# Weight-stationary fp32r pairs: the low weights' 256 columns first, and the low weights moved by 16 bytes

## The chip, the core and the metric

The kernel runs on one core of a Trainium2 chip. The metric is the device time of one execution in microseconds, as the median of several executions. TensorE is called PE here, VectorE DVE, ScalarE ACT, GpSimd POOL and the engine that issues most transfers SP. A line number such as L154 is a line of the kernel before.

## The reference

Two layers of a causal decoder over 256 positions of width 2048 (fp32): each is a sandwich-normed token mixer and a gated MLP of width 5632 with a causal depthwise convolution of width 3 on the gate.

```python
h = _rmsnorm(x, nrm[0]);  proj = h @ w_in_a[layer]       # layer 0: q, k, v, memory q
...                                                      # dilated attention, 12 heads; memory attention
x = x + _rmsnorm(heads @ w_o, norms[1])
u = _rmsnorm(x, norms[2]) @ w_up;  gate, val = jnp.split(u, 2, axis=-1)
acc = b_conv + ...                                       # 3 taps of the gate
x = x + _rmsnorm((jax.nn.silu(acc) * val) @ w_down, norms[3])
kv = _rmsnorm(x, g_kv) @ w_kv                            # shared by layer 1
q, qm = jnp.split(_rmsnorm(x, nrm[0]) @ w_in_b[lb], [SB_W], axis=-1)
...                                                      # stick-breaking attention, 12 heads; memory attention; same MLP
```

Nearly all of the work is in products of 256 rows with large weight matrices, each of which is read once.

## The kernel before

Each fp32 operand is split into a high and a low part in the type fp32r (hi is the rounded value, made by a cast on ACT at L669; lo the rest, made by a subtraction on DVE at L670). A product is hi·hi + hi·lo + lo·hi. There are two ways to compute it.

*Activations stationary* (`mm3`, L137): three matmuls of 512 moving columns; the weights move.

*Weights stationary* (`ws_mm`, L154): a feature tile of 128 outputs takes 16 k tiles of 128 rows. For each k tile the high weights `whi` are loaded into PE and multiplied with 512 moving columns, the high and the low activations beside each other (H below), and the low weights `wlo` with 256 columns, the high activations alone (L below). Both write one PSUM bank of 512 columns: H the whole of it, L the first 256. `ws_sum` then adds the two halves of the bank: a COPY on ACT (L165) and an addition on DVE (L166).

A feature tile arrives as one transfer (`raw`, 1 MB) and is split in two halves of 8 k tiles, each with a `whi` and a `wlo` of its own out of rings of four. Where a weight tile stands in memory is set by `halves`: tiles of 1088 elements (4352 bytes, a multiple of 256) of which 1024 are used from an offset on. `APART` sets these offsets for the weight-stationary tiles: 16 elements for whi and 4 for wlo, that is 64 and 16 bytes modulo 256. The other users of `halves`, `mem_kv` among them, use offset 0. The moving activations (`hset`) start at a multiple of 1024 bytes for every k tile.

In `ws_mm` H goes first and L second, apart from the last k tile of a bank and, in `ws_beside`, k tile 7 as well (`turn`), where L goes first. So in those places two L and then two H stand beside each other, or H ends the run.

Weight-stationary tiles are used in three places:

- `ws_pair` and `ws_tile`: 60 tiles one after another, the projections of queries and keys, the memory keys of layer 1, and the MLP groups that are done plainly.
- `ws_beside`: 96 tiles as a generator that `wide` steps through. `wide` computes a group of 512 gate and 512 value columns from sums of blocks (seven products instead of eight), eight units long, twelve such loops in all. Everything in it is recorded in program order (`pin`). In one unit PE runs: the first half of the tile (16 matmuls), products 1, 2 and 3 (nine matmuls at L137), the second half of the tile (16), products 7, 5, 6 and 4 (twelve). After a tile's second half come its `ws_sum` and then the two splits of the next tile, in this order on ACT and on DVE.
- `mem_kv`: the memory keys of layer 0, four banks at once, 64 k tiles with both weights at offset 0.

PE has one queue of instructions, in this order, and each matmul has a weight load of its own ahead of it (PEld in the profile). A matmul whose operand or bank isn't ready holds everything behind it.

Of the kernel before, what the change touches and what calls it, by code (L numbers as in the profile page):

```python
# [11 lines left out]
F32R = mybir.dt.float32r  # L12
# [5 lines left out]
P = 128  # L18
D = 2048
S = 256  # L20
# [4 lines left out]
KT = D // P  # L25
# [11 lines left out]
WIDE = (1, 3, 5, 7, 9)  # L37


APART = (16, 4)  # L40


QK_ORDER = []
# [5 lines left out]
class Body:  # L49
# [10 lines left out]
        return self.psp.tile([P, 512], F32, name="ps_" + tag, tag=tag, bufs=4)  # L60

    def small(self, n, dtype=F32):
        return self.sb.tile([P, n], dtype, name="small", tag="small", bufs=11)

    def sc(self, shape):
        return self.sb.tile(shape, F32, name="sc", tag="sc", bufs=4)
# [36 lines left out]
    def halves(self, at=(0, 0)):  # L103

        both = []
        for name, o in zip(("whi", "wlo"), at):
            both.append(self.sb.tile([P, 1088], F32R, name=name, tag=name, bufs=4)[:, o:o + 1024])
        return both

    def piece(self, src, cuts=1, store=None, between=None, at=(0, 0)):  # L110
# [31 lines left out]
    def ws_tile(self, out, src, h):  # L142
# [3 lines left out]
        self.step()  # L146
        for half, (whi, wlo) in enumerate(self.piece(src, at=APART)):
            for k in range(8):
                self.ws_mm(b, whi, wlo, k, h, half * 8 + k)
        self.ws_sum(out, b)  # L150

    def ws_mm(self, b, whi, wlo, k, h, kt, turn=None):

        mm = lambda *o, **kw: self.pin(self.nc.tensor.matmul(*o, **kw))  # L154
        ks = slice(k * P, (k + 1) * P)
        both, one = h[2][:, kt, :, :].rearrange("p a t -> p (a t)"), h[0][:, kt, :]
        last = kt == KT - 1 or kt == turn
        if not last:
            mm(b, whi[:, ks], both, start=kt == 0, stop=False)
        mm(b[:, 0:S], wlo[:, ks], one, start=False, stop=False)  # L160
        if last:
            mm(b, whi[:, ks], both, start=False, stop=kt == KT - 1)

    def ws_sum(self, out, b):
        self.pin(self.nc.scalar.copy(out, b[:, S:]))  # L165
        self.pin(self.nc.vector.tensor_add(out, b[:, 0:S], out))  # L166

    def ws_beside(self, out, src, h, done=None):


        raw = self.sb.tile([P, 2048], F32, name="raw", tag="raw", bufs=3)
        self.pin(self.nc.sync.dma_start(raw, src))
        parts = []
        for i in range(2):
            parts.append(self.halves(APART))
            self.split(*parts[i], raw[:, i * 1024:(i + 1) * 1024])
            yield
        b = self.bank("s")
        for half, (whi, wlo) in enumerate(parts):
            for k in range(8):  # L180
                self.ws_mm(b, whi, wlo, k, h, half * 8 + k, 7)
            yield
        self.ws_sum(out, b)
        if done:
            done()
# [474 lines left out]
    def rest_of(self, make):  # L660

        halves, rest = [], {}
        for u in range(0, 6, 2):
            rest[u] = lambda u=u: halves.append(make(5 + u // 2))
            rest[u + 1] = lambda: halves.pop()()
        return rest
# [732 lines left out]
```

## Time and profile before

| | |
|---|---|
| median of three executions | 2162.28 us (2161.65 to 2162.35) |
| profiled execution | 2161.4 us |
| span in it, first to last instruction | 2159.6 us |
| granted clock of PE, mean | 0.999 |
| busy: PE, PEld, DVE, ACT, POOL | 99%, 84%, 80%, 62%, 8% |
| moved by DMA | 538.83 MB, mean 250 GB/s |

The rows of the profile have a line, an engine, an operation, what is written and what is read, the shape, the number of instructions, their busy time and mean duration, and the idle time of the engine just before them with what ended it. In the timeline a row has its start and its duration, both in us from the span's start. Matmul records overlap: a matmul's recorded duration is longer than its distance to the next one's start, and a matmul that waits for its weights is recorded as running, so that idle time of PE doesn't always show as such.

### The profile page before, as it was taken

The numbers are of one execution on the slowest core, as the hardware profiler recorded it, in microseconds if no ns is written. First come the engines' busy times: TensorE is split into PE (matmuls) and PEld (weight loads), VectorE is DVE, ScalarE is ACT, GpSimd is POOL, SyncE is SP. The second block draws the span as 40 slices with busy tenths as digits, with TensorE's granted clock in tenths as the row PEclk, the third lists the DMA queues.
The fourth block names the chain that finished last, engine by engine and source line by source line (L and its number), as shares of the span: only waits on it lengthen the run. The fifth ranks groups of instructions, "written<-read, shape, count | busy, mean of one in ns | idle before, by whom it ended". The sixth has DMA issues, their size and how long they took to land.

```text
span 2159.6 us, 29240 instructions
## 1 busy us (share of the span) xinstructions
PE 2146.0 (99%) x10926; PEld 1823.1 (84%) x10926; DVE 1732.9 (80%) x2350; ACT 1328.2 (62%) x1896; POOL 175.4 (8%) x201
## 2 busy tenths in 40 slices
PE   9999999999999999999999999999999999999998
PEld 8888888888888888888888888878888888888887
DVE  7798867997887868788888978579978878687886
ACT  6666756666665666666675655456666656666563
POOL 0000001010101011010111000010101010110110
PEclk9999999999999999999999999999999999999999
DMA  9886557796979889797788744577969798897974
GB/s 371 252 262 247 174 187 259 223 284 220 299 234 283 266 236 303 225 290 257 264 268 260 256 165 177 192 234 229 275 233 288 235 283 269 236 303 222 290 247 184
DMA packets 111775, 538.83 MB, mean 250 GB/s; under 512 B 11280, under 2 KB 11664, under 8 KB 73488
## 3 DMA queue, kind: packets, MB, share of 16 engines
q1 hardware_dynamic: 75744, 445.66, 57.4%
q0 software_dynamic: 35744, 91.24, 20.9%
q8 instruction: 86, 1.41, 0.2%
q14 instruction: 57, 0.47, 0.1%
q10 hardware_dynamic: 144, 0.06, 0.0%
HBM read 510.17 MB, written 26.74 MB: 249 GB/s over the span
## 4 chain that ended last, share of the span: by engine, by line
PE 97%; DVE 1%; issue 1%; ACT 0%; DMA 0%; POOL 0%; POOLq 0%; DVEq 0%; SPq 0%; ACTq 0%
PE ps_g L137 40%; PE ps_s L154 25%; PE ps_g L154 15%; PE ps_s L137 12%; PE ps_s L961 1%; PE ps_s L287 1%; PE ps_s L363 0%; PE ps_s L390 0%; DMA sh<-in_uw_dram 0%; DVE wlo L670 0%; PE ps_s L1082 0%; PE ps_s L495 0%; PE ps_s L477 0%; PE ps_s L535 0%; PE ps_s L434 0%
## 5 line engine op out<-in xcount | busy, mean ns | idle before, releaser
L670 DVE TENSOR_TENSOR wlo<-raw,whi 128x1024 fp32r<-128x1024 f32 (+1 forms) x758 | 855.2, 1151 | 245.7 <-ACT whi L669 232.4
L669 ACT CAST whi<-raw 128x1024 fp32r<-128x1024 f32 (+1 forms) x758 | 742.8, 995 | 386.9 <-PE ps_g L137 145.8
L154 PE MATMUL ps_s<-h,whi 128*128 128x512 f32 x1600 | 573.3, 393 | 0.0
L137 PE MATMUL ps_g<-whi,sh 128*128 128x512 f32 x1488 | 462.0, 392 | 0.5 <-ACT sc L779 0.5
L154 PE MATMUL ps_s<-h,wlo 128*128 128x256 f32 x1600 | 416.2, 280 | 0.1
L154 PEld LDWEIGHTS ps_s<-h,whi 128*128 128x128 f32 x1600 | 300.3, 188 | 54.2
L154 PE MATMUL ps_g<-h,whi 128*128 128x512 f32 x960 | 338.0, 396 | 0.8 <-DVE h L277 0.8
L137 PEld LDWEIGHTS ps_g<-whi,sh 128*128 128x128 f32 x1488 | 277.4, 188 | 57.6 <-ACT sc L779 1.4
L154 PEld LDWEIGHTS ps_s<-h,wlo 128*128 128x128 f32 x1600 | 300.7, 188 | 23.3 <-DVE wlo L670 0.7
L137 PE MATMUL ps_g<-wlo,sh 128*128 128x512 f32 x744 | 290.3, 390 | 0.0
L154 PE MATMUL ps_g<-h,wlo 128*128 128x256 f32 x960 | 259.1, 280 | 0.0
L670 DVE TENSOR_TENSOR x<-sh,x 128x1024 fp32r<-128x1024 f32 x192 | 227.1, 1220 | 0.2 <-ACT x L669 0.2
L137 PE MATMUL ps_g<-whi,h 128*128 128x512 f32 x688 | 214.2, 393 | 0.0
L154 PEld LDWEIGHTS ps_g<-h,whi 128*128 128x128 f32 x960 | 178.6, 188 | 36.4 <-DVE h L277 1.3
L669 ACT CAST x<-sh 128x1024 fp32r<-128x1024 f32 x192 | 193.4, 1051 | 2.1 <-DVE sh L715 2.1
L154 PEld LDWEIGHTS ps_g<-h,wlo 128*128 128x128 f32 x960 | 180.5, 188 | 3.9
L165 ACT COPY qk<-ps_s 128x256 f32<-128x256 f32 x96 | 35.8, 373 | 223.5 <-PE ps_s L154 223.5
L137 PEld LDWEIGHTS ps_g<-wlo,sh 128*128 128x128 f32 x744 | 139.7, 188 | 29.3
L137 PE MATMUL ps_s<-x,h 128*128 128x512 f32 x552 | 155.4, 390 | 0.0
L677 POOL DMA_DIRECT2D sh<-in_uw_dram x80 | 98.4, 1229 | 659.4 <-DMA sh<-in_uw_dram 226.0
L137 PE MATMUL ps_g<-x,h 128*128 128x512 f32 x528 | 149.8, 392 | 0.0
L137 PEld LDWEIGHTS ps_g<-whi,h 128*128 128x128 f32 x688 | 129.1, 189 | 23.5
(215 smaller groups left out, 2255.4 us busy)
## 6 DMA issues: line engine op xcount, KB each, us to landing
raw<-in_up_dram SPq DMA_DIRECT2D x96, 1024.0 KB, 6.9
raw<-in_dn_dram SPq DMA_DIRECT2D x88, 1024.0 KB, 5.5
raw<-in_uw_dram SPq DMA_DIRECT2D x80, 768.0 KB, 8.2
sh<-in_uw_dram SPq DMA_DIRECT2D x80, 512.0 KB, 8.3
sh<-in_uw_dram POOLq DMA_DIRECT2D x80, 512.0 KB, 10.4
raw<-in_wqk_a_dram SPq DMA_DIRECT2D x24, 1024.0 KB, 5.0
yout<-sh POOLq DMA_DIRECT2D x32, 512.0 KB, 8.6
raw<-in_wo_b_dram SPq DMA_DIRECT2D x16, 1024.0 KB, 4.9
```

What stands on the lines that cost most here:

```text
L137: mm = lambda *o, **k: self.pin(self.nc.tensor.matmul(*o, **k))
L154: mm = lambda *o, **kw: self.pin(self.nc.tensor.matmul(*o, **kw))
L165: self.pin(self.nc.scalar.copy(out, b[:, S:]))
L287: self.nc.tensor.transpose(b[:, k * S + t * P:k * S + (t + 1) * P], self.x[:, t, kt * P:(kt + 1) * P], self.ident)
L669: high = self.pin(self.nc.scalar.copy(hi, of))
L670: low = self.pin(self.nc.vector.tensor_sub(lo, of, hi.bitcast(F32)))
L677: self.nc.gpsimd.dma_start(d.rearrange("p (a n) -> p a n", a=2), src[u][:, 1536:].unsqueeze(1).to_broadcast([P, 2, 512]), accum_op=ALU.add)
L961: nc.tensor.transpose(b[:, j * S + t * P:j * S + (t + 1) * P], of[t][:, f:f + P], self.ident)
```

## The change

In `ws_mm` L now goes first and H second at every k tile; `turn` is gone. Since L, which writes only half of the bank, opens it, the first k tile of a bank can't use one H over both halves: it is done as L and two matmuls of 256 columns with the same `whi`, one per half of the bank. That is one matmul and one weight load more for each of 160 banks: 60 and 96 tiles and the four of `mem_kv`.

`APART` becomes (16, 0): wlo starts at 0 modulo 256. The wlo tiles need no room for an offset any more and shrink to 1024 elements; the ring `small` grows from 11 to 16 buffers. With that `R`, `Rs`, `Rm` and the `sc` tiles, which lie behind them, start at 128 modulo 256 instead of 224.

```diff
-APART = (16, 4)
+APART = (16, 0)
...
-        return self.sb.tile([P, n], dtype, name="small", tag="small", bufs=11)
+        return self.sb.tile([P, n], dtype, name="small", tag="small", bufs=16)
...
-        for name, o in zip(("whi", "wlo"), at):
-            both.append(self.sb.tile([P, 1088], F32R, name=name, tag=name, bufs=4)[:, o:o + 1024])
+        for name, n, o in zip(("whi", "wlo"), (1088, 1024), at):
+            both.append(self.sb.tile([P, n], F32R, name=name, tag=name, bufs=4)[:, o:o + 1024])
...
-    def ws_mm(self, b, whi, wlo, k, h, kt, turn=None):
+    def ws_mm(self, b, whi, wlo, k, h, kt):
...
         both, one = h[2][:, kt, :, :].rearrange("p a t -> p (a t)"), h[0][:, kt, :]
-        last = kt == KT - 1 or kt == turn
-        if not last:
-            mm(b, whi[:, ks], both, start=kt == 0, stop=False)
-        mm(b[:, 0:S], wlo[:, ks], one, start=False, stop=False)
-        if last:
+        mm(b[:, 0:S], wlo[:, ks], one, start=kt == 0, stop=False)
+        if kt:
             mm(b, whi[:, ks], both, start=False, stop=kt == KT - 1)
+        else:
+            for i in range(2):
+                mm(b[:, i * S:(i + 1) * S], whi[:, ks], h[i][:, kt, :], start=False, stop=False)
...
-                self.ws_mm(b, whi, wlo, k, h, half * 8 + k, 7)
+                self.ws_mm(b, whi, wlo, k, h, half * 8 + k)
```

PE at the top of a tile in the first loop of `wide`, before: the last products of the unit before, then the tile's first half. The names in brackets are the semaphores that a row waits for, counted by the engine named.

```order
L137 MATMUL ps_g<-x,h_507 128x512 x2
L137 MATMUL ps_s<-x,h_86 128x512 x3
L154 MATMUL ps_s<-h_86,whi 128x512 [waits DVE_49,Activation_49]
L154 MATMUL ps_s<-h_86,wlo 128x256 [waits DVE_49]
L154 MATMUL ps_s<-h_86,whi 128x512
L154 MATMUL ps_s<-h_86,wlo 128x256
```

PE at the same place with the change:

```order
L137 MATMUL ps_g<-x,h_511 128x512 x2
L137 MATMUL ps_s<-x,h_86 128x512 x3
L155 MATMUL ps_s<-h_86,wlo 128x256 [waits DVE_49]
L155 MATMUL ps_s<-h_86,whi 128x256 [waits Activation_49]
L155 MATMUL ps_s<-h_86,whi 128x256
L155 MATMUL ps_s<-h_86,wlo 128x256
```

The wait for DVE's `wlo` has moved from the tile's second matmul to its first, where it also covers the bank that DVE's addition of an earlier tile has freed.

PE at the end of a tile's first half in the same loop, before, with the products that follow:

```order
L154 MATMUL ps_s<-h_86,whi 128x512
L154 MATMUL ps_s<-h_86,wlo 128x256
L154 MATMUL ps_s<-h_86,whi 128x512
L154 MATMUL ps_s<-h_86,wlo 128x256 x2
L154 MATMUL ps_s<-h_86,whi 128x512
L137 MATMUL ps_g<-whi,h_86 128x512 x2
```

PE at the same place with the change:

```order
L155 MATMUL ps_s<-h_86,wlo 128x256
L155 MATMUL ps_s<-h_86,whi 128x512
L155 MATMUL ps_s<-h_86,wlo 128x256
L155 MATMUL ps_s<-h_86,whi 128x512
L137 MATMUL ps_g<-whi,h_86 128x512 x2
```

The turn with two neighbouring L is gone, and the half alternates to its end. The order of the splits and sums on ACT and DVE in these loops is as it was.

## The prediction

> **What bounds the kernel now.** I read the page first: the busy shares, then the costliest groups.
>
> ```profile
> PE 2146.0 (99%) x10926; PEld 1823.1 (84%) x10926; DVE 1732.9 (80%) x2350; ACT 1328.2 (62%) x1896; POOL 175.4 (8%) x201
> L154 PE MATMUL ps_s<-h,whi 128*128 128x512 f32 x1600 | 573.3, 393 | 0.0
> L154 PE MATMUL ps_g<-h,whi 128*128 128x512 f32 x960 | 338.0, 396 | 0.8 <-DVE h L277 0.8
> ```
>
> TensorE (PE) is the bound: busy for 99% of the span, with idle times of a microsecond at most in these groups. The change touches its 2560 pairs (1600 in ps_s, 960 in ps_g) of a 512-column matmul on whi (H) and a 256-column one on wlo (L). The mean durations (393 ns for H) overlap, since matmuls are pipelined; what counts is the distance between starts, which only the timeline shows. Here is one tile of the loop of `wide`, PE, ACT and DVE interleaved from its timeline (start, duration):
>
> ```profile
> 599.18 0.40 PE L154 MATMUL ps_s<-h,whi 128*128 128x512 f32 x1
> ...
> 599.61 0.37 ACT L165 COPY qk<-ps_s 128x256 f32<-128x256 f32 x1 [3.07 <-PE ps_s L154]
> 599.88 1.05 ACT L669 CAST whi<-raw 128x1024 fp32r<-128x1024 f32 x1
> 600.96 1.23 DVE L670 TENSOR_TENSOR wlo<-raw,whi 128x1024 fp32r<-128x1024 f32 x1 [0.52 <-ACT whi L669]
> ...
> 602.15 0.40 PE L154 MATMUL ps_s<-h,whi 128*128 128x512 f32 x1
> 602.24 0.19 PEld L154 LDWEIGHTS ps_s<-h,wlo 128*128 128x128 f32 x1
> ...
> 602.51 0.39 PE L154 MATMUL ps_s<-h,whi 128*128 128x512 f32 x1
> ...
> 604.21 0.39 PE L154 MATMUL ps_s<-h,whi 128*128 128x512 f32 x1
> ...
> 604.90 0.63 PE L137 MATMUL ps_g<-whi,h 128*128 128x512 f32 x2
> ...
> 606.28 0.62 PE L137 MATMUL ps_s<-whi,h 128*128 128x512 f32 x2
> ...
> 606.96 0.39 PE L154 MATMUL ps_s<-h,whi 128*128 128x512 f32 x1
> ...
> 609.05 0.39 PE L154 MATMUL ps_s<-h,whi 128*128 128x512 f32 x1
> ...
> 609.51 0.40 PE L154 MATMUL ps_s<-h,whi 128*128 128x512 f32 x1
> ```
>
> Three things are to be seen. First, the pitch of a pair has two values: (604.21 - 602.51) / 5 = 0.340 us in the first half, (609.05 - 606.96) / 6 = 0.348 in the second, where the first pair is the slowest (0.347 for the later ones), with the same instructions and the same addresses modulo 256. Of the 96 first halves 54 run at the short pitch (2.75 us for all 16 matmuls), the others and all second halves at the long one (2.79). The products at L137, nine of 512 columns, take 606.96 - 604.90 = 2.06 us, the last three of them (606.96 - 606.28) / 3 = 0.227 each: what PE gives steadily for 512 columns.
>
> Second, a chain through ACT and DVE closes on PE at the top of each tile. The last H of the tile before starts at 599.18; the COPY of its sum (L165) follows at 599.61, the cast to whi behind it at 599.88, the subtraction that makes wlo at 600.96. It ends at 602.19, and the load of wlo starts at 602.24: 3.06 us after the last H. PE meanwhile has twelve products, and its first H starts at 602.15. So wlo comes 0.09 us after PE has begun the tile, and it costs next to nothing, because H, which needs only whi, goes first and covers it. No idle time is reported, since the matmul ahead is still running. This is so at 84 tiles: the eight of each of the twelve `wide` loops but the first. First and last of them:
>
> ```profile
> 106.36 0.18 PEld L154 LDWEIGHTS ps_s<-h,wlo 128*128 128x128 f32 x1
> ...
> 2073.37 0.19 PEld L154 LDWEIGHTS ps_s<-h,wlo 128*128 128x128 f32 x1
> ```
>
> Third, one of the 84 shows what a load that PE does wait for costs:
>
> ```profile
> 1200.27 0.19 PEld L154 LDWEIGHTS ps_s<-h,wlo 128*128 128x128 f32 x1 [0.55 <-DVE wlo L670]
> 1200.37 0.19 PEld L154 LDWEIGHTS ps_s<-h,whi 128*128 128x128 f32 x1
> ```
>
> The next load starts when the matmul of the first one does, so a matmul follows its own load by 0.10 us when PE stands idle.
>
> **The change part by part.** *The wait at the top of a tile.* L now leads, so PE's first instruction is the one that needs wlo; ACT and DVE keep their order. Queued behind it are the tile's whole first half and all later PE work. The load can't start before 602.24, its matmul not before 602.34, and PE was ready at 602.15: 0.19 us of idle PE. It is not caught up within the tile, since the next chain starts from PE's own last H: T + 3.06 + 0.10, where PE's twelve products had needed 2.97. 84 x 0.19 = +16.0 us. A faster product stage would only lengthen the wait. Below nothing this term can't go, since DVE's end is the same; above, 0.24 a tile (+20) if those products shed 0.05.
>
> *The pitch of a pair.* Only wlo moves, from 16 bytes modulo 256 to 0; whi stays at 64, the moving operand at 0. No row shows that pair of places. The nearest rows: under H the load is now one at 0, as under the L137 products: 0.227. Under L the load is still whi at 64, 0.113 to 0.117 (what is left of 0.340 and 0.347 after H's 0.227 and 0.230). That gives 0.340 to 0.344, and I take 0.342. The ends: a row with both weights at 0, from the memory keys at the start, where H and L alternate,
>
> ```profile
> 12.81 0.40 PE L154 MATMUL ps_s<-h,whi 128*128 128x512 f32 x1
> ...
> 17.76 0.40 PE L154 MATMUL ps_s<-h,whi 128*128 128x512 f32 x1
> ```
>
> is (17.76 - 12.81) / 14 = 0.353, the upper end; the lower is H at 0.227 plus a bare weight load, 0.10: 0.33. The load and the stream evidently disturb each other, and the place decides by how much.
>
> *Turns go, a third matmul comes.* Each half of a tile now alternates throughout; the two neighbouring L near its end and the slower H beside them vanish. Once a tile, L, H, H of 256 columns stand in for a pair: no less than 0.113 each, as an L at the short pitch, and with their own loads to place some more than 0.117; say 0.35 for the three, 0.01 over a pair, times 160 banks = 1.6 us, in the sums below.
>
> *Halves in the loops.* First half: 0.35 + 7 x 0.342 = 2.744 against a mean of 2.77 (54 at 2.75, 42 near 2.79). Second, up to its last H: 7 x 0.342 + 0.115 = 2.509 against 609.51 - 606.96 = 2.55. Together -0.067; x 96 tiles = -6.4 us.
>
> *Tiles of* `ws_pair`, 60 of them, 960 pairs, one after another:
>
> ```profile
> 388.88 0.48 PE L154 MATMUL ps_g<-h,whi 128*128 128x512 f32 x1
> ...
> 414.00 0.62 PE L137 MATMUL ps_g<-whi,h 128*128 128x512 f32 x2
> ...
> 206.53 0.28 PE L154 MATMUL ps_g<-h,wlo 128*128 128x256 f32 x1
> ...
> 211.75 0.38 PE L431 MATMUL ps_s<-qk 128*128 128x128 f32 x2
> ```
>
> Here 72 pairs take 25.12 us, 0.349 each; the tile at 206 runs at the short pitch (5.22 us from its first L, for 15 pairs and one L: (5.22 - 0.115) / 15 = 0.340). Mean about 0.347. Now 0.342 and 0.01 a tile: 960 x (-0.005) + 0.6 = -4.2 us. wlo is ready there some microseconds before its load, so leading with it costs nothing, unless DVE's backlog eats that lead, as it might in the stretch from 388 to 414.
>
> *The rest* costs nothing: the merged wait for the freed bank (one semaphore now covers bank and wlo) lay under the matmul ahead; the 64 pairs of the memory keys keep their place; the larger ring `small` and the shifted addresses of `sc`, `R`, `Rm` touch short ACT and DVE work under a PE that is 99% busy. Where DVE's share of the chain at 600.96 got shorter or longer by that, the wait would move with it; nothing shows it.
>
> Sum: +16.0 - 6.4 - 4.2 = +5.4 us. The profiled execution took 2161.4 (span 2159.6), 0.9 under the median of 2162.28; 2161.4 + 5.4 = 2166.8, so about 2167.
>
> **The rivals.** One nanosecond of pitch is worth 2.4 us (15 pairs of 96 tiles and 960 pairs), and the wait stays in all of these but the second.
>
> *The pitch falls below what was seen*, as 0.333: (0.342 - 0.333) x 2400 = 21.6 less, 2145; faster than before below some 0.338, where the pairs' gain passes the wait. For it: the spread from 0.353 to 0.340 by place and phase alone says that part of the pitch is disturbance. Against it: the products at L137 stay at 0.227. The Trainium skill, "TensorE: Matmul & The Clock Gate", section "Back-to-back issue gap", gives N / 2.4 + 2.5 ns for matmuls in a row, 216 and 109 ns, a pair of 0.325; by that estimate the sum would be some 40 us lower. The trace's 0.227 contradicts it for this data type.
>
> *The wait is not there*, because ACT and DVE reach their end of the chain sooner: 16 less, 2151. Against it: their order stands and each step of the chain is its engine's own work, 0.37, 1.05 and 1.23 us.
>
> *Every pair runs at 0.340, with transients gone*: 0.002 x 2400 = 4.8 less, 2162, no change. For it: whole halves hold that pitch.
>
> *The placement does nothing*: pairs stay at 0.347 and the wait is bare: +5 x 2.4 = 12 more, 2179. For it: second halves hold 0.347 whatever runs beside them, and the 54 short first halves all follow a late wlo load, which the new order takes away. The Trainium skill, "TensorE: Matmul & The Clock Gate", section "Step-by-step: what each phase is for", says that the moving operand and the weights have read ports of their own, so that addresses should not matter; the three pitches above speak against it.
>
> *wlo at 0 disturbs as in the memory keys*: 0.353, 11 x 2.4 = 26 more, 2193.
>
> **How the numbers follow.** Forecast (0.340 to 0.344, full wait; 2163 to 2172) 0.35; all at 0.340 0.18; below that 0.18; no wait 0.03; placement without effect 0.18; 0.353 0.08. A change of 0.2%, 4.3 us (2158 to 2166.6), is about what can be told here. Faster: the case below 0.340, the one without the wait and a little of the even one, 0.24. Same: most of the even one and two fifths of the forecast, 0.29. Slower: the rest, 0.47. The range from 2148 to 2184 leaves out the 0.353 case and the lower third or so of the fast one, about 0.16. The forecast's own range is 2163 to 2172.
>
> **What would show it.** Right: loads of wlo at the head of the 84 tiles with an idle PE of some 0.2 us released by DVE wlo L670 (some 16 us in the list of waits); the step from last H to the tile's first matmul at 3.16 instead of 2.97; pairs at 0.342 in both halves. Wrong: no such wait, which would mean that the chain shortened; pairs at 0.333 or 0.353.

## The result and the profile after

The changed kernel took 2173.48 us in the median of four executions (2173.32 to 2175.37), the kernel before 2162.32 beside it (2161.65 to 2162.64): 1.0053 times, 95% interval 1.0039 to 1.0067. It is slower, by 11 us where 5 were forecast: inside the whole range of 2148 to 2184, but outside the likeliest case's own range of 2163 to 2172. In the profiled executions the span went from 2159.6 to 2171.7 us, the granted clock of TensorE from 0.999 to 0.998; the clock is not the cause, since an execution of the changed kernel at 0.999 took 2173.32. Line numbers of the kernel after are one higher: `ws_mm` is L155, COPY L166, the cast to whi L670, wlo L671.

From the page of the kernel after: busy time of the engines, then the groups of the pairs and of the loads of wlo (busy time, mean ns of one, idle time ahead and what ended it).

```profile
PE 2158.9 (99%) x11086; PEld 1825.9 (84%) x11086; DVE 1734.8 (80%) x2350; ACT 1330.1 (61%) x1896; POOL 175.6 (8%) x201
L155 PE MATMUL ps_s<-h,whi 128*128 128x512 f32 (+1 forms) x1700 | 558.9, 378 | 0.0
L155 PEld LDWEIGHTS ps_s<-h,wlo 128*128 128x128 f32 x1600 | 300.9, 188 | 36.0 <-DVE wlo L671 31.7
```

PE's share hides the loss: a matmul that waits for its weights counts as busy. Only the row of the loads has it. The list of waits of the weight loads says the same of the kernel after (us in total, times, longest),

```profile
PEld ps_s L155 <- DVE wlo L671: 31.7, 84, 0.7
```

and of the kernel before:

```profile
PEld ps_s L154 <- DVE wlo L670: 0.7, 2, 0.5
```

84 waits, as many as the tiles that are not the first of a loop. The timeline of the kernel after shows one of them, with ACT and DVE between PE's rows:

```profile
602.64 0.39 PE L155 MATMUL ps_s<-h,whi 128*128 128x512 f32 x1
...
603.07 0.37 ACT L166 COPY qk<-ps_s 128x256 f32<-128x256 f32 x1 [3.00 <-PE ps_s L155]
603.34 2.00 ACT L670 CAST whi<-raw 128x1024 fp32r<-128x1024 f32 x2
...
604.42 2.36 DVE L671 TENSOR_TENSOR wlo<-raw,whi 128x1024 fp32r<-128x1024 f32 x2 [0.52 <-ACT whi L670]
...
604.91 0.84 PE L137 MATMUL ps_s<-x,h 128*128 128x512 f32 x3
...
605.70 0.19 PEld L155 LDWEIGHTS ps_s<-h,wlo 128*128 128x128 f32 x1 [0.37 <-DVE wlo L671]
605.70 0.39 PE L155 MATMUL ps_s<-h,wlo 128*128 128x256 f32 x1
605.81 0.31 PEld L155 LDWEIGHTS ps_s<-h,whi 128*128 128x128 f32 x2
605.92 0.40 PE L155 MATMUL ps_s<-h,whi 128*128 128x256 f32 x2
```

From the tile's last H at 602.64 to the load at 605.70 are 3.06 us, the same chain as before. The first L is recorded as starting with its load. By the prediction's reading it really starts with the next load, at 605.81; the next matmul, at 605.92, then follows it by 0.11, the usual distance behind an L. That is 3.17 us after the last H, against 2.97 to the first matmul before. The 0.37 in brackets is idle time of the load queue; part of it still lay under the last product, so the listed 31.7 us are about twice the loss.

The pitch of a pair (the distance from one H to the next) of the kernel after, in a first half that had no wait (first tile of a loop), in the first half behind the wait shown above, and in a second half:

```profile
543.36 0.40 PE L155 MATMUL ps_s<-h,whi 128*128 128x512 f32 x1
...
545.46 0.40 PE L155 MATMUL ps_s<-h,whi 128*128 128x512 f32 x1
...
606.63 0.39 PE L155 MATMUL ps_s<-h,whi 128*128 128x512 f32 x1
...
608.33 0.39 PE L155 MATMUL ps_s<-h,whi 128*128 128x512 f32 x1
...
610.71 0.39 PE L155 MATMUL ps_s<-h,whi 128*128 128x512 f32 x1
...
613.09 0.39 PE L155 MATMUL ps_s<-h,whi 128*128 128x512 f32 x1
```

(545.46 - 543.36) / 6 = 0.350 us, (608.33 - 606.63) / 5 = 0.340 and (613.09 - 610.71) / 7 = 0.340. The same instructions with the same places in memory run at two paces. Of the 84 first halves behind a wait 67 settle at 0.340 and 17 at 0.350; the 12 without a wait all settle at 0.350. A tile of `ws_pair` in the same kernel, with its third matmul just ahead:

```profile
391.53 0.40 PE L155 MATMUL ps_g<-h,whi 128*128 128x512 f32 x1
...
393.28 0.39 PE L155 MATMUL ps_g<-h,whi 128*128 128x512 f32 x1
```

(393.28 - 391.53) / 5 = 0.350 again. Of the 35 long stretches of such tiles 26 run at 0.350, 7 at 0.340 and 2 at both; all 96 second halves run at 0.340.

Where the 12.1 us of span went, by the distances between the starts of matmuls, summed by stage over both whole traces. A tile's head is its first H in the kernel before, its first L and the first part of H in the kernel after:

| stage | forecast, us | measured, us |
|---|---|---|
| twelve products and head of the next tile, 84 (the wait) | +16.0 | +16.6 |
| the rest of the first halves, 96 | -2.5 | +0.3 |
| second halves, 96 | -3.9 | -6.4 |
| `ws_pair` and its like, 35 stretches | -4.2 | +2.4 |
| nine products | 0 | -1.3 |
| elsewhere | 0 | +0.5 |
| sum | +5.4 | +12.1 |

### The profile page after: what moved, and what is told of

It reads as the page before. It is cut to its first block, busy times and chain, and to the rows that moved or that the text cites. A ratio compares the mean times of both kernels' runs of the same rounds, so it can differ in the third digit from the quotient of the medians.

```text
span 2171.7 us, 29474 instructions
## 1 busy us (share of the span) xinstructions
PE 2158.9 (99%) x11086; PEld 1825.9 (84%) x11086; DVE 1734.8 (80%) x2350; ACT 1330.1 (61%) x1896; POOL 175.6 (8%) x201
## 4 chain that ended last, share of the span: by engine, by line
PE 98%; issue 1%; DVE 1%; ACT 0%; DMA 0%; POOL 0%; POOLq 0%; DVEq 0%; SPq 0%; ACTq 0%
PE ps_g L137 40%; PE ps_s L155 26%; PE ps_g L155 15%; PE ps_s L137 12%; PE ps_s L962 1%; PE ps_s L288 1%; PE ps_s L364 0%; DMA sh<-in_uw_dram 0%; PE ps_s L391 0%; PE ps_s L1083 0%; PE ps_s L496 0%; PE ps_s L478 0%; PE ps_s L435 0%; DVE wlo L671 0%; PE ps_s L536 0%
## 5 line engine op out<-in xcount | busy, mean ns | idle before, releaser
L671 DVE TENSOR_TENSOR wlo<-raw,whi 128x1024 fp32r<-128x1024 f32 (+1 forms) x758 | 855.4, 1151 | 249.2 <-ACT whi L670 243.0
L670 ACT CAST whi<-raw 128x1024 fp32r<-128x1024 f32 (+1 forms) x758 | 743.9, 996 | 399.9 <-PE ps_g L137 146.1
L155 PE MATMUL ps_s<-h,whi 128*128 128x512 f32 (+1 forms) x1700 | 558.9, 378 | 0.0
L155 PE MATMUL ps_s<-h,wlo 128*128 128x256 f32 x1600 | 452.9, 283 | 0.3 <-DVE wlo L671 0.3
L155 PEld LDWEIGHTS ps_s<-h,whi 128*128 128x128 f32 x1700 | 312.4, 188 | 56.9
L155 PE MATMUL ps_g<-h,whi 128*128 128x512 f32 (+1 forms) x1020 | 337.9, 382 | 0.0
L155 PEld LDWEIGHTS ps_s<-h,wlo 128*128 128x128 f32 x1600 | 300.9, 188 | 36.0 <-DVE wlo L671 31.7
L155 PE MATMUL ps_g<-h,wlo 128*128 128x256 f32 x960 | 273.4, 285 | 0.0
L671 DVE TENSOR_TENSOR x<-sh,x 128x1024 fp32r<-128x1024 f32 x192 | 227.1, 1219 | 0.1
L155 PEld LDWEIGHTS ps_g<-h,whi 128*128 128x128 f32 x1020 | 188.2, 189 | 36.8 <-DVE h L278 0.2
L670 ACT CAST x<-sh 128x1024 fp32r<-128x1024 f32 x192 | 193.4, 1051 | 1.4 <-DVE sh L716 1.4
L155 PEld LDWEIGHTS ps_g<-h,wlo 128*128 128x128 f32 x960 | 182.2, 190 | 0.8 <-ACT h L277 0.2
L166 ACT COPY qk<-ps_s 128x256 f32<-128x256 f32 x96 | 35.8, 373 | 222.2 <-PE ps_s L155 222.2
```

What stands on the lines that cost most here:

```text
L670: high = self.pin(self.nc.scalar.copy(hi, of))
L671: low = self.pin(self.nc.vector.tensor_sub(lo, of, hi.bitcast(F32)))
```

## The experiments

Every kernel below is compared with the kernel before on the same chip; its median there was 2161.70 us beside the first four and 2163.05 beside the last four.

### The places alone, and the order alone

The kernel before with wlo at 0 modulo 256, H first as it was:

```diff
-APART = (16, 4)
+APART = (16, 0)
...
-        return self.sb.tile([P, n], dtype, name="small", tag="small", bufs=11)
+        return self.sb.tile([P, n], dtype, name="small", tag="small", bufs=16)
...
+        for name, n, o in zip(("whi", "wlo"), (1088, 1024), at):
```

> The kernel before with the new places alone (wlo at 0 modulo 256, its tiles 1024 wide, small with 16 buffers), H first and the turns as before. Theory A (the change lost its time by the wait for wlo at the top of 84 tiles, 17 us, and won some 6 back by pitch): no wait, so not slower than before; 2150 to 2164, lower if second halves fall from 2.79 to 2.72 us by the place alone, 2162 if that needs L first. Rival B (the places or the shifted addresses are what costs): 2168 to 2178.

2161.99 us, ratio 1.0002 (0.9993 to 1.0012): nothing in the sum. Inside, the pitch did move, both ways. A second half and the first half behind it:

```profile
101.22 0.39 PE L154 MATMUL ps_s<-h,whi 128*128 128x512 f32 x1
...
102.92 0.39 PE L154 MATMUL ps_s<-h,whi 128*128 128x512 f32 x1
...
106.70 0.40 PE L154 MATMUL ps_s<-h,whi 128*128 128x512 f32 x1
...
108.45 0.40 PE L154 MATMUL ps_s<-h,whi 128*128 128x512 f32 x1
```

(102.92 - 101.22) / 5 = 0.340 in the second half, (108.45 - 106.70) / 5 = 0.350 in the first. All 96 second halves run at 0.340 here (2.747 us), 34 of the first halves too, and the other 62 at 0.350 and above. So wlo at 0 doesn't set a pace: the same instructions run at more than one, and what picks it must lie in what surrounds them.

The kernel after with wlo back at 16 and the rings as before:

```diff
-APART = (16, 0)
+APART = (16, 4)
...
-        return self.sb.tile([P, n], dtype, name="small", tag="small", bufs=16)
+        return self.sb.tile([P, n], dtype, name="small", tag="small", bufs=11)
...
-        for name, n, o in zip(("whi", "wlo"), (1088, 1024), at):
+        for name, n, o in zip(("whi", "wlo"), (1088, 1088), at):
```

> The changed kernel with the old places (wlo at 16 modulo 256, small with 11 buffers): L first and the third matmul alone. Theory A: the 84 waits of 0.20 us stay, 17 us; 2172 to 2180, the upper end if second halves stay at 2.79 us. Rival B (the places cost): 2155 to 2163.

2168.34 us, ratio 1.0032 (1.0021 to 1.0044). The order alone makes the kernel slower, though by less than the 2172 that was the least expected of it. Its waits are those of the kernel after:

```profile
PEld ps_s L155 <- DVE wlo L671: 32.0, 85, 0.7
```

Second halves take 2.720 us here too (16 matmuls). So either edit alone brings their pairs to 0.340, the place of wlo or L going first; the order takes away the turn as well, 2.720 instead of 2.747. The `ws_pair` stretches took 2.9 us less than before, where the kernel after took 2.4 more.

### The wait taken away, by splitting earlier

In `wide`, the split of the next tile's first half is recorded ahead of the sum of this tile, instead of behind it, so that neither COPY nor PE's last H stands in the chain any more. (The expectation below puts the split ahead of the second half too; in the edit it stands between the half's matmuls and the sum, which leaves ACT and DVE the same order.) First on the kernel after:

```diff
             next(b)
+            if more:
+                next(after)
             next(b, None)
             if more:
                 next(after)
-                next(after)
```

> The changed kernel with one edit in wide: the first of the next tile's two splits is recorded before this tile's second half and sum, so that whi and wlo of the next first half are made while ACT would wait for PE. PE's order stays. Theory A: the 84 waits go, minus 17 us, 2155 to 2158. Rival B (the loss is in pitch or the third matmul): 2172 to 2174, the waits gone from the list but the time back elsewhere.

2156.62 us, ratio 0.9979 (0.9969 to 0.9988): 17 us below the kernel after (spans 2155.1 and 2171.7), where the wait was put at 16.6. The list of waits has one entry left of the 84:

```profile
PEld ps_s L155 <- DVE wlo L671: 0.4, 1, 0.4
```

and the last H, the next tile's first L, and the pairs behind its third matmul stand so:

```profile
103.74 0.39 PE L155 MATMUL ps_s<-h,whi 128*128 128x512 f32 x1
...
106.68 0.28 PE L155 MATMUL ps_s<-h,wlo 128*128 128x256 f32 x1
...
107.14 0.40 PE L155 MATMUL ps_s<-h,whi 128*128 128x512 f32 x1
...
109.24 0.40 PE L155 MATMUL ps_s<-h,whi 128*128 128x512 f32 x1
```

106.68 - 103.74 = 2.94, which is thirteen times 0.226: PE goes through without a pause. The first half still runs at (109.24 - 107.14) / 6 = 0.350, in all 96 tiles (2.793 us each). So that pace is not a consequence of the wait. On the contrary, with the wait 67 of them had run at 0.340: by the starts of the matmuls the wait's stage takes 19.3 us less than in the kernel after, the rest of the first halves 2.9 more and the nine products 1.4 more.

The same edit on the kernel before:

> The kernel before with the same early split. Theory A: its late wlo cost almost nothing, so no gain; if the late load is what puts 54 first halves on the short pitch, they go to 2.79 us and it is 2 us slower, 2164 to 2165; otherwise 2162. Rival B': the late wlo did cost PE time that its record hides, 0.09 us at 84 tiles: 2154 to 2156.

2161.98 us, ratio 1.0001 (0.9991 to 1.0010): nothing. There the late load was covered by H, so there was nothing to win. Yet the 54 short first halves are gone: first and second halves take 2.787 us in the median, as this one does (start of its first and of its last H),

```profile
106.81 0.39 PE L154 MATMUL ps_s<-h,whi 128*128 128x512 f32 x1
...
109.36 0.40 PE L154 MATMUL ps_s<-h,whi 128*128 128x512 f32 x1
```

2.55 us as in the prediction's row of a second half. That costs 2.0 us in the rest of the first halves; the 2164 to 2165 expected of it didn't come, and the profiled span is only 0.8 us longer, the rest being won in small amounts elsewhere. With the late load of wlo the short halves went too. The edit moves the whole split in time, though, so that the load itself had put them on the 0.340 pace is likely, but not shown.

### The old places with the wait away

The order of the kernel after, wlo at 16, and the early split, that is the second and the third edit together:

> L first and the third matmul, the early split, but the places of before (wlo at 16 modulo 256). Theory P (behind the third matmul the pair's pitch settles by the place of wlo: 0.340 with 16, 0.351 with 0): first halves 2.73 instead of 2.79 us, 96 x 0.06 = 6 us less than with wlo at 0, some more in ws_pair; 2146 to 2151. Rival (the place of wlo makes no difference once the wait is gone): 2156 to 2158.

2144.78 us, ratio 0.9914 (0.9899 to 0.9929): the fastest of all, faster than both kernels of the change, and a little below the 2146 to 2151 expected. Behind the third matmul the pace is 0.340 after two pairs:

```profile
106.48 0.39 PE L155 MATMUL ps_s<-h,whi 128*128 128x512 f32 x1
...
108.18 0.39 PE L155 MATMUL ps_s<-h,whi 128*128 128x512 f32 x1
```

(108.18 - 106.48) / 5 = 0.340. The only differences to the run at 2156.62 are the place of wlo, by 16 bytes, and the rings, and they are worth about 12 us; the two were not tried apart. Of these, first halves (2.733 against 2.793 in the median) are 5.5 in sum, `ws_pair` 4.8, and the nine products (2.040 against 2.061) 2.0; that is 12.3, of which 0.9 is lost elsewhere (spans 2155.1 and 2143.7).

### Where the good pace of the second half comes from

The kernel before, with L first in k tiles 8 to 15 of `ws_beside` and nowhere else; no third matmul is needed there, and the tile's top keeps H first.

```diff
-        last = kt == KT - 1 or kt == turn
+        last = kt == KT - 1 or (turn is not None and kt >= turn)
```

> The kernel before, wlo at 16, with L first in the second halves of ws_beside alone (k tiles 8 to 15): no wait moves there, no third matmul. Theory A's gain by itself: second halves 2.72 instead of 2.79 and the products behind them 2.72 instead of 2.74: 96 x 0.067 + 86 x 0.02 = 8 us less, 2153 to 2155. Rival (L first has no gain without the new places or the third matmul): 2161 to 2163.

2155.24 us, ratio 0.9962 (0.9948 to 0.9976). All second halves take 2.720 us:

```profile
101.31 0.39 PE L154 MATMUL ps_s<-h,whi 128*128 128x512 f32 x1
...
103.69 0.39 PE L154 MATMUL ps_s<-h,whi 128*128 128x512 f32 x1
```

(103.69 - 101.31) / 7 = 0.340. This is the gain of the change's second halves without its wait, in one line of code: the second half's wlo is ready when it leads. One thing went with it: of the 55 first halves at 0.340 (the prediction's 54 and one behind a long wait) only 16 are left, though their wlo still comes after PE's first H. So a late load alone doesn't bring that pace.

### What the third matmul does to the pace

The early split on the kernel after (wlo at 0), with the bank opened as H of the second 256 columns, L, H of the first 256, instead of L, H, H:

```diff
-        mm(b[:, 0:S], wlo[:, ks], one, start=kt == 0, stop=False)
+        if kt == 0:
+            mm(b[:, S:], whi[:, ks], h[1][:, kt, :], start=True, stop=False)
+        mm(b[:, 0:S], wlo[:, ks], one, start=False, stop=False)
...
-            for i in range(2):
-                mm(b[:, i * S:(i + 1) * S], whi[:, ks], h[i][:, kt, :], start=False, stop=False)
+            mm(b[:, 0:S], whi[:, ks], one, start=False, stop=False)
```

> early_after with the bank opened in another order: the high weights on the second 256 columns, L, the high weights on the first 256. As many matmuls and loads. Theory Q (the order of the three sets the phase of all pairs behind them): first halves move away from 2.79, to 2.73 at best: 2149 to 2151 or, if they settle worse, 2157 to 2160. Rival (three short matmuls shift the phase in any order, the place of wlo decides): within 1 us of early_after.

2148.61 us, ratio 0.9932 (0.9918 to 0.9947): 8 us below L, H, H at the same places (2156.62). Its first half:

```profile
106.39 0.39 PE L155 MATMUL ps_s<-h,whi 128*128 128x512 f32 x1
...
108.43 0.39 PE L155 MATMUL ps_s<-h,whi 128*128 128x512 f32 x1
```

(108.43 - 106.39) / 6 = 0.340. The same number of matmuls in another order of three, and the fourteen that follow run 3% faster to the half's end, in 94 of the 96 first halves. So it is the entry L, H, H, with wlo at 0 and no wait, that leads to 0.350 there. In `ws_pair` this kernel's stretches are mixed still.

### Both weights at 0

The early split on the kernel after, with `APART = (0, 0)`:

> early_after with both weights at 0 modulo 256. Theory R (whi at 64 is what lets its load pass under L without disturbance): pairs towards the 0.353 of the memory keys, 6 to 13 ns more on 2400 pairs, 2165 to 2187, and second halves no longer at 2.72. Rival (the order alone gives the second halves their 2.72): 2153 to 2160.

2178.66 us, ratio 1.0072 (1.0057 to 1.0087), 22 us above the same kernel with whi at 64 (spans 2176.1 and 2155.1). A second half:

```profile
101.27 0.40 PE L155 MATMUL ps_s<-h,whi 128*128 128x512 f32 x1
...
103.39 0.40 PE L155 MATMUL ps_s<-h,whi 128*128 128x512 f32 x1
```

(103.39 - 101.27) / 6 = 0.353, the pitch of the memory keys, in every half, whether L, H, H or L, H opens it; some tiles of `ws_pair` hold 0.347. The place of whi matters too, and more.

## Why the prediction was right in sign and short in size

*The wait* was right: its mechanism, its 84 places and nearly its price. Last H to first L was put at 3.16 and measured at 3.17; the stage lost 16.6 us against 16.0 (16.6 / 84 = 0.20 a tile instead of 0.19). Taking the wait away made the kernel 17 us faster. What the prediction said of the list of waits, some 16 us, was wrong: the list has 31.7, since it counts the load queue's idle time under a running matmul.

*The pitch of a pair* is the step that failed. The prediction took one value for all pairs, 0.342, because the place of the weights was to decide it. The runs show steady paces, among which the place, the order of the first matmuls and the time of the split select. With wlo at 0 a second half settles at 0.340, better than forecast (-6.4 us instead of -3.9). Pairs behind the third matmul settle either at 0.340 or at 0.350, slower than the 0.347 of the kernel before: 29 of the 96 first halves and 26 of the 35 stretches of `ws_pair` are at 0.350. So first halves gained nothing where 2.5 us were forecast, and the term for `ws_pair`, -4.2, came out at +2.4. That term is the largest of the mis-sized ones: off by 6.6 us, about the whole 6.7 between forecast and sum. That the others cancel (+0.6, +2.8, -2.5, -1.3, +0.5) is luck. The third matmul itself cost what was said, about one distance of 0.113 to 0.120; its price is in the pairs that follow.

The rivals: no half or tile fell below 0.340, so the faster case was wrong. By the formula of the Trainium skill, "TensorE: Matmul & The Clock Gate", section "Back-to-back issue gap", a pair would take an estimated 0.325, which no run here came near. The prediction took the formula as one for matmuls in a row, as the section's heading has it; the section's text calls it that of a single matmul and puts a sustained stream of 512 columns at about 131 ns, where the products here take 227 ns. *The wait is not there* was wrong for this change, but its conditions came true with the early split. *Every pair at 0.340* holds in all second halves, but not in all first halves, nor in `ws_pair`. *The placement does nothing* was wrong: 2144.78, 2156.62 and 2178.66 us are three runs of the same order of PE's matmuls with the weights at (64, 16), (64, 0) and (0, 0) bytes; the last two differ in nothing else, the first in the rings too. The Trainium skill, "TensorE: Matmul & The Clock Gate", section "Step-by-step: what each phase is for", gives the weights and the moving operand ports of their own; here the weights' address changes the pace of the whole. As the pace of every half 0.353 came only with whi at 0 as well.

A check of the sum the other way: the prediction's case with all pairs at 0.340 was 2162, with the wait of 16 in it. Without the wait that is 2146, and the kernel without it that has 0.340 in 94 of the 96 first halves and in nearly all second ones measured 2144.78. That it comes so near is partly luck, since nearly half of its `ws_pair` pairs are at 0.347 or above.

What stays open: why a pace, once entered, persists over the seven pairs of a half or the fifteen of a tile. The runs show that place, order and the time of the split select it, not through what; the place of wlo and the rings moved by the same edit were not told apart. A single 512-column H in place of the third matmul's two parts was not tried, so that the third matmul is needed at all is not shown. In part of `ws_pair` both paces occur in one kernel, and what ahead of each tile decides was not traced.

## What to carry to other kernels

Before the operand that comes last is moved to the head of a stage, follow the chain that makes it: an operation that goes first is the one whose inputs must be ready, and a load that came 0.09 us late for nothing cost 0.2 us each time it led. Move its producers as well, or change the order only where the operand has long been there (here the second half, 7.8 us with one line). For a pitch of back-to-back matmuls measure each way into the stretch apart, with the places held fixed; a mean over a mixture of two paces predicts neither.

## What the hardware showed that was not expected

Over a half or a tile, pairs of a 512- and a 256-column matmul mostly held one of four mean paces, 0.340, 0.347, 0.350 or 0.353 us. 0.340 is 1.5 times the 0.227 of a 512-column matmul in the products, and nothing went below it. Which pace a first half took, counted in the traces by the median of its pairs, depends on place, order and timing together:

| kernel | first matmuls; wlo at | at 0.340, of 84 tiles behind another | of 12 first tiles of a loop |
|---|---|---|---|
| before | H, L; 16 | 55 | 0 |
| `second_half` | H, L; 16 | 16 | 0 |
| `early_before`, early split | H, L; 16 | 0 | 0 |
| `place_only` | H, L; 0 | 25 | 9 |
| after | L, H, H; 0 | 67 | 0 |
| `early_after`, early split | L, H, H; 0 | 0 | 0 |
| `order_only` | L, H, H; 16 | 31 | 10 |
| `early_old_places`, early split | L, H, H; 16 | 84 | 10 |
| `hlh`, early split | H, L, H; 0 | 83 | 11 |

With L, H, H the early split takes the good pace away where wlo stands at 0 (67 to 0) and brings it where wlo stands at 16 (31 to 84). Three matmuls of 256 columns in another order (L, H, H or H, L, H) changed the pace of the fourteen that follow from 0.350 to 0.340 per pair.
